# Layer 0's output projection: four of six chunk pairs as block products over all 16 k-tiles

## The chip, the core and the metric

The kernel runs as one program on one core of a Trainium2 chip. A core has five engines with queues of their own, which run in order: TensorE (PE; its weight loads are shown as PEld), VectorE (DVE), ScalarE (ACT), GpSimd (POOL) and SyncE (SP), which here does nothing but issue DMA transfers. The metric is the device time of one execution in microseconds (us); several executions are timed and the median is given. Beside them one execution was recorded by the hardware profiler; all rows below come from it.

## The reference

One step of a two-layer backbone over 640 tokens (128 context tokens, 512 latent tokens), 2048 features, fp32. Each layer normalises and modulates the input, projects it to branch inputs and gates, runs two branches (layer 0: windowed attention and gated linear attention; layer 1: neighbourhood attention and spatial gating), multiplies by the gate, and projects back:

```
for l in range(DEPTH):                       # DEPTH = 2
    shift, scale, gate = modulation(c, ada_w[l], ada_b[l])
    h = rms_norm(x, norm_g[l]) * (1.0 + scale[:, None]) + shift[:, None]
    y, _ = even_mixer(h, ...)   or   odd_mixer(h, ...)
    x = x + gate[:, None] * (y @ w_out[l])   # w_out[l]: 2048 x 2048
y_sample = rms_norm(x, final_norm_g)
```

The change concerns `y @ w_out[0]` alone.

## The kernel before, in words

**Layout.** Activations are feature-major: a tensor of 2048 features by 640 tokens is 16 k-tiles of 128 partitions x 640 columns. The tokens fall into two halves of 320. Every fp32 operand is split into a high and a low part in a reduced fp32 format (`acth`/`actl` for activations, `whi`/`wlo` for weights), and each fp32 product is three matmuls: high x high, low x high, high x low. Weights arrive raw (`wraw`, `rs`), ScalarE writes `whi`, GpSimd or now and then VectorE writes `wlo`, four k-tiles (128x512) at a time, into a ring that holds five such units.

**The output projection** has 16 output chunks of 128 features. Chunks 0 and 1 are done as a plain pair (`kpair`, 2 x 16 k-tiles x 2 halves x 3 = 192 matmuls). Chunks 2 to 13 are six pairs done by `spair`. Chunks 14 and 15 are a plain pair again, which in layer 0 runs into layer 1's input projection.

**Block products.** A pair has 2 chunks x 2 k-halves (k-tiles 0 to 7 and 8 to 15) on the weight side and 2 k-halves x 2 token halves on the activation side, a 2x2 by 2x2 block product. `spair` forms it with 7 products instead of 8 (Strassen's scheme): four of them use sums of activations (f = 0, 1, 2, and `t3`, which overwrites the second token half of `acth`/`actl` for k-tiles 0 to 7), four use sums of weight blocks (S1 to S4), which VectorE forms in `rs`/`wraw`. There are two forms:

- The full form (`ns` = NS = 8): all 16 k-tiles in block products; 7 products x 8 k-tiles x 3 = 168 matmuls, 14 weight units, 8 sums of 128x512 on VectorE.
- The short form (`ns` = NR = 4): k-tiles 0 to 3 and 8 to 11 in block products, 4 to 7 and 12 to 15 plainly; 7 x 4 x 3 + 4 units x 4 k-tiles x 2 halves x 3 = 84 + 96 = 180 matmuls, 11 weight units, 4 sums.

The order of a pair's steps (`steps`, line 656):

```
todo = "A11' A11 A12 A12' S1' S1 S4' S4 S2 S2' S3 S3' A22 A22'".split()      # full, first of a row
return [*names("A11"), *a[:1], *names("A12"), *a[1:], *names("S1", "S2", "S4"), *b[:1], *names("S3"), *b[1:], *names("A22")]   # short
```

A prime means the far half of the k-tiles; a and b are the plain units of the two chunks.

**Near and far sums.** `fold` prepares the activation sums. The near ones (k-tiles 0 to 3 with 8 to 11) are made by VectorE and kept on chip in `eh`/`el`. The far ones (4 to 7 with 12 to 15) are made by GpSimd and ScalarE (`far` in `fold`), stored to `far_dram`, and read back one sum at a time into four slots in `tail`; the slots lie where k-tiles 12 to 15 of the residual `Y` would be, and `turn_tail` swaps the two uses. When a product has read a slot for the last time, the transfer that brings the slot's next sum is issued (`far_load`). `t3` and the overwritten halves of `acth`/`actl` go through DRAM as well (`t3_dram`, shown as `t_dram`; `bh_dram`, `bl_dram`): `third` in `fold` brings `t3` in, `unfold` restores the old content for the plain pair that follows. If `fold` gets no third flag, it makes no far sums and all this is done for k-tiles 0 to 3 alone.

**What sets the order.** The program is written out by a planner in Python: `Pace` keeps an estimated clock for each engine; while TensorE's matmuls are written in fixed order, pending work of the other engines (evacuations, splits, weight sums, fold steps) is put into their queues when the planner thinks that its inputs are there. All DMA transfers go through SP's queue. A background task, `ada_task`, computes the modulation vectors (`part`, `partg`) from 64 weight tiles of 128x2048 (`ada`) on VectorE, piece by piece through four buffers `adas`, wherever the planner sees room; its outputs are needed by layer 1's input (jobs `s1`, `1`) and by layer 1's output projection (job `g1`).

The pairs are formed in `program`; `pairs(n, short, used)` marks the first `short` of `n` pairs as short and gives the last short one the flag `used`, which tells `fold` that k-tiles 4 to 7 are no longer read plainly:

```
acts.extend(("s", [c[2 * i], c[2 * i + 1], NR if i < short else NS, used if i == short - 1 else None, None]) for i in range(n))
pairs((KT - 4) // 2, SHORT[l], f"us{l}")
```

Layer 1's output projection already has two short pairs and four full ones, with a fold that makes far sums.

Of the kernel before, what the change touches and what calls it, by code (L numbers as in the profile page):

```python
# [41 lines left out]
LEAD, FIRST = 2, 8  # L42
ORDER = "k0 v0 q0 q1 k1 v1 q2 q3 g0 q4 q5 g1 q6 g2 q7".split()
GHOSTS = 12, 13
SHORT = 6, 2


class Pace:
# [187 lines left out]
class Trunk:  # L236
# [2099 lines left out]
    def program(self):  # L2336
# [23 lines left out]
        def pairs(n, short=0, used=None):  # L2360

            c = [acts.pop()[1] for _ in range(2 * n)][::-1]
            acts.extend(("s", [c[2 * i], c[2 * i + 1], NR if i < short else NS, used if i == short - 1 else None, None]) for i in range(n))

        def do(f):
            acts.append(("f", f))
# [203 lines left out]
        def to_y(l, free, cs):  # L2570

            for k in ORDERS[l]:
                y = self.yt(k) if l else Y[:, k, :]
                yield from self.wait(f"{free}:{k}", *(f"evac{c}" for c in cs if k in ORDERS[l][-2:]))
                yield from self.until(y)
                yield from self.calm(self.calms[0])
                self.act_plain(k, y, f"y{l}:{k}")
                yield

        def out_proj(l, xsrc, sp):  # L2580
            for i, f in enumerate(range(KT)):
# [4 lines left out]
                elif i == KT - 3:  # L2586
                    pairs((KT - 4) // 2, SHORT[l], f"us{l}")
            do(lambda: self.turn_tail(False))
# [10 lines left out]
        cs = pair("k", ORDERS[0], None, "fe")  # L2599
        k = acts.pop()  # L2600
        do(lambda: self.spawn(to_y(0, "fe", cs)))
        do(lambda: self.fold("y0", "uo0", None))
        acts.append(k)
        do(lambda: (self.need("ada_g0"), self.spawn(scales())))

# [456 lines left out]
```

## Time and profile before

| | us |
|---|---|
| three timed executions | 2086.84, 2087.51, 2090.91 (median 2087.51) |
| profiled execution | 2084.72 |
| its span, first to last instruction | 2082.9 |
| TensorE busy in the span | 2036.0 (98%) |
| layer 0's output projection, about | 840 to 1031 |
| layer 1's output projection, about | 1850 to 2070 |

The profiled execution spends 1.8 us outside the span. A stretch is named by microseconds from the span's start. "Busy" of TensorE counts overlapping matmuls once; a matmul of 320 columns is recorded with some 310 ns, but the next one starts 147 ns later. In a list of waits each row gives who waited, for whom, the total, how often, and the longest.

### The profile page before, as it was taken

The numbers are of one execution on the slowest core, as the hardware profiler recorded it, in microseconds if no ns is written. First come the engines' busy times: TensorE is split into PE (matmuls) and PEld (weight loads), VectorE is DVE, ScalarE is ACT, GpSimd is POOL, SyncE is SP. The second block draws the span as 40 slices with busy tenths as digits, with TensorE's granted clock in tenths as the row PEclk, the third lists the DMA queues.
The fourth block names the chain that finished last, engine by engine and source line by source line (L and its number), as shares of the span: only waits on it lengthen the run. The fifth ranks groups of instructions, "written<-read, shape, count | busy, mean of one in ns | idle before, by whom it ended". The sixth has DMA issues, their size and how long they took to land. (4 is left out here: it accounts for less than half of the span.)

```text
span 2082.9 us, 38915 instructions
## 1 busy us (share of the span) xinstructions
PE 2036.0 (98%) x13930; PEld 1963.8 (94%) x13930; DVE 1503.7 (72%) x3465; ACT 959.6 (46%) x1995; POOL 1097.9 (53%) x830
## 2 busy tenths in 40 slices
PE   7999999999999999999999999999999999999996
PEld 4788999999999999999999999999999999999995
DVE  1447788887888777788767778987785667676465
ACT  3344444353334454544454544555554545454443
POOL 3447243233222223466556675756666567658783
PEclk9999999999999999999999999999999999999998
DMA  9954333345554434776648856756665575567756
GB/s 374 359 173 134 124 119 124 122 137 184 159 169 142 128 127 132 232 253 221 205 132 274 269 192 231 253 198 213 219 197 192 179 258 190 191 222 244 249 186 217
DMA packets 215874, 412.52 MB, mean 198 GB/s; under 512 B 25664, under 2 KB 88320, under 8 KB 215680
## 3 DMA queue, kind: packets, MB, share of 16 engines
q1 hardware_dynamic: 214208, 408.43, 58.9%
q8 instruction: 109, 1.79, 0.3%
q10 hardware_dynamic: 1472, 1.61, 0.2%
q14 instruction: 85, 0.70, 0.1%
HBM read 368.88 MB, written 38.45 MB: 196 GB/s over the span
## 5 line engine op out<-in xcount | busy, mean ns | idle before, releaser
L396 PE MATMUL bank<-acth,whi 128*128 128x320 f32 (+1 forms) x3112 | 956.8, 319 | 8.8 <-DVE arena L210 3.0
L396 PE MATMUL bank<-acth,wlo 128*128 128x320 f32 (+1 forms) x3112 | 929.9, 311 | 3.3 <-POOL wlo L210 3.1
L396 PE MATMUL bank<-actl,whi 128*128 128x320 f32 (+1 forms) x3112 | 928.8, 310 | 0.0
L210 POOL TENSOR_TENSOR wlo<-wraw,whi 128x512 fp32r<-128x512 f32 x363 | 505.5, 1399 | 663.5 <-ACT whi L210 596.1
L396 PEld LDWEIGHTS bank<-acth,whi 128*128 128x128 f32 x3112 | 578.9, 189 | 26.1 <-issue 11.2
L396 PEld LDWEIGHTS bank<-acth,wlo 128*128 128x128 f32 x3112 | 578.6, 189 | 4.7 <-POOL wlo L210 4.6
L396 PEld LDWEIGHTS bank<-actl,whi 128*128 128x128 f32 x3112 | 579.0, 189 | 1.8
L210 POOL TENSOR_TENSOR wlo<-rs,whi 128x512 fp32r<-128x512 f32 x292 | 407.5, 1408 | 185.2 <-ACT whi L210 162.3
L210 ACT ACTIVATE whi<-wraw 128x512 fp32r<-128x512 f32 x393 | 241.0, 624 | 163.0 <-PE bank L396 87.4
L210 ACT ACTIVATE whi<-rs 128x512 fp32r<-128x512 f32 x329 | 201.1, 625 | 104.2 <-PE bank L396 60.9
L210 DVE CUSTOM_DVE_ANT_0 adas<-adas,bank,partg 128x256 bf16<-128x256 f32 (+1 forms) x320 | 178.0, 556 | 19.2 <-DMA adas<-ada_g 10.0
L396 PE MATMUL bank<-tail,whi 128*128 128x322 f32 (+1 forms) x672 | 152.0, 313 | 0.1
L210 ACT ACTIVATE arena<-arena,bc 128x128 f32<-128x128 f32 (+3 forms) x167 | 83.6, 519 | 143.7 <-DVE bc L210 95.2
L396 PE MATMUL bank<-eh,whi 128*128 128x322 f32 (+1 forms) x444 | 138.8, 313 | 0.0
L396 PE MATMUL bank<-el,whi 128*128 128x322 f32 (+1 forms) x444 | 137.8, 310 | 0.0
L396 PE MATMUL bank<-eh,wlo 128*128 128x322 f32 (+1 forms) x444 | 137.7, 310 | 0.0
L210 DVE TENSOR_TENSOR bank<-bank,sums 128x320 f32<-128x320 f32 (+1 forms) x162 | 76.6, 493 | 66.9 <-PE bank L396 58.5
L210 ACT ACTIVATE Y<-bank 128x128 f32<-128x128 f32 (+5 forms) x134 | 52.2, 411 | 138.8 <-PE bank L396 73.0
L210 ACT ACTIVATE sums<-bank 128x320 f32<-128x320 f32 (+1 forms) x125 | 54.5, 436 | 127.3 <-PE bank L396 118.9
L396 PEld LDWEIGHTS bank<-tail,whi 128*128 128x128 f32 x672 | 112.2, 189 | 0.5 <-DMA tail<-far_dram 0.4
L210 DVE TENSOR_TENSOR rs<-rs 128x512 f32<-128x512 f32 x83 | 85.5, 1036 | 31.8 <-POOL wlo L210 31.4
L396 PE MATMUL bank<-tail,wlo 128*128 128x322 f32 (+1 forms) x336 | 103.8, 309 | 0.0
(227 smaller groups left out, 2870.5 us busy)
## 6 DMA issues: line engine op xcount, KB each, us to landing
tail<-far_dram SPq DMA_DIRECT2D x196, 322.0 KB, 4.0
wraw<-w_even SPq DMA_DIRECT2D x176, 256.0 KB, 3.1
adas<-ada_g SPq DMA_DIRECT2D x128, 256.0 KB, 3.8
adas<-ada SPq DMA_DIRECT2D x128, 256.0 KB, 3.7
rs<-w_odd SPq DMA_DIRECT2D x63, 512.0 KB, 5.7
wraw<-w_odd SPq DMA_DIRECT2D x37, 512.0 KB, 5.6
more<-ada SPq DMA_DIRECT2D x36, 512.0 KB, 7.5
rs<-w_out SPq DMA_DIRECT2D x30, 512.0 KB, 5.7
```

The source lines that it names most:

```text
L210: return f(*args, **kw)
L396: self.nc.tensor.matmul(out, lhsT, rhs, start=start, stop=stop, **kw)
```

## The change

The table entry `SHORT` for layer 0 goes from 6 to 2, and layer 0's `fold` gets the flag `us0` as its third argument, so that it makes far sums:

```
-SHORT = 6, 2
+SHORT = 2, 2
...
-        do(lambda: self.fold("y0", "uo0", None))
+        do(lambda: self.fold("y0", "uo0", "us0"))
```

The third to sixth pairs (chunks 6 to 13) become full. The instructions of the planner's other work move with them.

GpSimd's queue at the start of layer 0's output projection, while chunks 0 and 1 are multiplied (`Y` and `tail` hold the gated branch outputs there, `stage` is a buffer of the fold):

```order
-L210 TENSOR_TENSOR wlo<-wraw,whi 128x512 x151
-L210 TENSOR_TENSOR wlo<-rs_7760,whi 128x512
-L210 TENSOR_TENSOR wlo<-wraw,whi 128x512 x2
+L210 TENSOR_TENSOR wlo<-wraw,whi 128x512 x146
+L210 TENSOR_TENSOR Y<-Y 128x320
+L210 TENSOR_TENSOR Y<-tail_81,Y 128x320
+L210 TENSOR_TENSOR wlo<-wraw,whi 128x512
+L210 TENSOR_TENSOR Y<-Y,stage_7761 128x320
+L210 TENSOR_TENSOR tail_81<-tail_81,Y 128x320
+L210 TENSOR_TENSOR wlo<-wraw,whi 128x512
```

The far sums (128x320) stand between the low parts of the weights; there are 32 of them, spread over the plain pair and the two short pairs, where before there was none.

SP's queue in the third pair (`tail<-far_dram` are the slots' next sums, `rs` and `wraw` the weights, `adas` the background task):

```order
+L434 DMA tail_8872<-far_dram 128x2x320 x2
+L434 DMA adas<-ada 128x512
+L434 DMA rs_7760<-w_out 128x1024
 L434 DMA adas<-crow_s 128x512 x2
-L434 DMA adas<-ada 128x512 x3
+L434 DMA rs_7760<-w_out 128x1024
+L434 DMA tail_8872<-far_dram 128x2x320 x2
+L434 DMA adas<-ada 128x512
+L434 DMA tail_8872<-far_dram 128x2x320 x2
+L434 DMA wraw<-w_out 128x1024
+L434 DMA rs_7760<-w_out 128x1024
+L434 DMA adas<-ada 128x512 x2
```

The slot transfers stand between the weights and the background task's pieces, of which fewer are left in this stretch.

## Rows read from the trace of the kernel before

**Rows 1.** The page, part 1: busy us, share of the span, instructions.

```profile
PE 2036.0 (98%) x13930; PEld 1963.8 (94%) x13930; DVE 1503.7 (72%) x3465; ACT 959.6 (46%) x1995; POOL 1097.9 (53%) x830
```

**Rows 2.** Windows: stretch, length, busy (count) by engine, clock, DMA share, GB/s.

```profile
core 0: us, PE busy (x) PEld busy (x) DVE busy (x) ACT busy (x) POOL busy (x), PEclk, DMA share, GB/s
860.00:1030.00 170.00, 170.00 (x1156) 170.00 (x1155) 134.42 (x383) 76.08 (x147) 111.43 (x91) 1.00 0.72 231
...
1864.00:1940.00 76.00, 76.00 (x519) 76.00 (x518) 46.07 (x67) 34.23 (x70) 62.96 (x55) 1.00 0.77 250
1940.00:1960.00 20.00, 19.36 (x129) 18.76 (x129) 10.13 (x15) 7.07 (x13) 15.93 (x12) 1.00 0.76 241
1960.00:2040.00 80.00, 80.00 (x546) 79.97 (x545) 48.38 (x63) 35.58 (x69) 63.12 (x49) 1.00 0.68 222
```

**Rows 3.** Windows: the background task beside layer 1's attention heads, and the heads alone.

```profile
1300.00:1560.00 260.00, 259.62 (x1757) 255.01 (x1756) 212.99 (x623) 132.31 (x295) 166.61 (x122) 1.00 0.64 218
1560.00:1700.00 140.00, 140.00 (x948) 137.57 (x947) 87.89 (x205) 72.93 (x159) 81.66 (x62) 1.00 0.61 209
```

**Rows 4.** Windows: 20 us with the DMA engines full.

```profile
1100.00:1120.00 20.00, 20.00 (x137) 20.00 (x136) 7.91 (x14) 5.73 (x12) 9.09 (x9) 1.00 0.99 342
```

**Rows 5.** TensorE's waits, 1864 to 2040.

```profile
PE bank L396 <- ACT sums L210: 0.5, 1, 0.5
```

**Rows 6.** TensorE's waits, 1045 to 1090.

```profile
PE bank L396 <- DVE tail L210: 2.4, 2, 1.9
PE bank L396 <- POOL wlo L210: 0.4, 1, 0.4
```

**Rows 7.** DMA, 860 to 1030: queue, packets, MB, share; then issues, KB, us to landing.

```profile
q1 hardware_dynamic: 21028, 38.97, 71.7%
...
adas<-ada SPq DMA_DIRECT2D x34, 256.0 KB, 4.6
...
adas<-ada_g SPq DMA_DIRECT2D x19, 256.0 KB, 4.2
...
adas<-crow_s SPq DMA_DIRECT2D x7, 256.0 KB, 4.7
```

**Rows 8.** DMA, 1864 to 2040.

```profile
q1 hardware_dynamic: 26018, 41.36, 72.2%
...
tail<-far_dram SPq DMA_DIRECT2D x36, 320.0 KB, 4.3
...
far_dram<-Y SPq DMA_DIRECT2D x12, 160.0 KB, 3.4
```

**Rows 9.** Transfers to and from `far_dram`, 1864 to 2040: ns min/median/max, first and last start.

```profile
L434 SPq DMA_DIRECT2D tail<-far_dram x36: 359/419/1076, 1920.2 to 2018.0; - x36
...
  PEld bank L396: 0.4, 1
...
DMA to landing us min/median/max: 1.9/4.0/7.3
```

**Rows 10.** TensorE in order of time, layer 1's first full pair.

```profile
1947.63 0.46 PE L396 MATMUL bank<-tail,whi 128*128 128x320 f32 x2
```

**Rows 11.** VectorE by form, 1864 to 2040: busy us, mean ns, idle before.

```profile
L210 DVE TENSOR_TENSOR rs<-rs 128x512 f32<-128x512 f32 x13 | 14.8, 1147 | 13.3 <-POOL wlo L210 13.2
L210 DVE TENSOR_TENSOR wlo<-rs,whi 128x512 fp32r<-128x512 f32 x14 | 14.3, 1030 | 8.2 <-ACT whi L210 8.1
```

**Rows 12.** The background task on VectorE, 860 to 1030: ns min/median/max, first and last start.

```profile
L210 DVE CUSTOM_DVE_ANT_0 adas<-adas,bank,part x74: 735/748/751, 870.9 to 959.4; 128x512 bf16<-128x512 f32 x74
```

**Rows 13.** The same, 1400 to 1800.

```profile
L210 DVE CUSTOM_DVE_ANT_0 adas<-adas,bank,partg x71: 462/476/484, 1404.0 to 1552.1; 128x256 bf16<-128x256 f32 x71
```

## The prediction

> **What bounds the kernel now.** The page's busy shares come first: TensorE is busy for 98% of the span, no other engine for more than 72% [rows 1]. The window over layer 0's output projection, where the change lies, says more: in 860 to 1030 TensorE is busy for all of 170 us, at the full clock, with 1156 matmuls, so one every 170/1156 = 0.1471 us [rows 2]. A matmul less there is worth 0.147 us as long as nothing else becomes late. The others have room, but not much: VectorE 134 of 170 us, GpSimd 111, the DMA engines 72%. The third look is at a twin: layer 1's output projection already has two short and four full pairs. In 1864 to 2040 TensorE stands still there for 0.64 us in all, in the one window 1940 to 1960 [rows 2], and the list of waits has one entry, 0.5 us [rows 5]. The twin lacks what layer 0 has beside it, the background task of modulation vectors: in 860 to 1030 that task brings 34 + 19 + 7 pieces of 256 KB [rows 7].
>
> **Matmuls, -7.1 us.** A short pair has 180 matmuls, a full one 168. Four pairs by 12 by 0.1471 us [rows 2] is 7.06 us. The order of the changed program has 48 matmuls fewer, so the change does what it says, and I give no chance to its doing nothing. The weight loads go with their matmuls.
>
> **The first full pair, +1.1 us.** The twin has 129 matmuls in 1940 to 1960, and 546 in the 80 us behind it, 136.5 in 20 us [rows 2]: 7.5 fewer, 1.1 us. TensorE waits there for a copy of ScalarE to free a bank [rows 5] and for a slot transfer, 0.4 us on the weight-load queue [rows 9]. Layer 0's third pair gets the same steps, so I take the same: bounds 0 (there is only this one such place) and 2.2 (both waits twice as long).
>
> **The fold of the far sums, 0.** 32 subtractions of 128x320 come on GpSimd, with their splits on ScalarE and 32 stores. What they must not miss is the third pair's first product with a slot. In the twin the first slot transfer is issued at 1920.2 [rows 9] and the first matmul that reads a slot starts at 1947.63 [rows 10]: 27 us of cover. In layer 0 the same steps stand between the same pairs, with the background task's pieces among them. If the cover is gone, each us later costs one; more than 27 us I do not expect.
>
> **VectorE and GpSimd, 0.** A full pair needs four more weight sums and three more weight units than a short one: 16 sums and 12 units in all, a sum at 1147 ns and a low part on VectorE at 1030 ns [rows 11]. The order gives VectorE 13 low parts more and GpSimd one fewer over the whole program, so VectorE gets 16 x 1.15 + 13 x 1.03 = 32 us of work more. What gives way is the background task: of its operations in this stage the order keeps 82, where 143 stood. The 61 that leave are of the shorter kind, 61 x 0.48 = 29 us [rows 13]. VectorE's load in the stage stays about where it is. GpSimd has 32 subtractions more, near 1 us each, on 111 of 170 us: about 80%, and the twin has 63 of 76 and 63 of 80 us, with TensorE standing still for 0.64 us [rows 2]. Zero, then, with 2 us as the upper bound (five waits for a low part of 0.4 us [rows 6]).
>
> **The DMA engines, +3.3 us.** This is where I see the doubt. 38.97 MB at a share of 71.7% in 170 us [rows 7] is 320 GB/s with the engines full; the twin's 41.36 MB at 72.2% in 176 us [rows 8] gives 325. The change adds, by the order: 36 slot transfers of 328 KB (11.8 MB), 24 stores of far sums, 8 of `t3`, and 8 each way of the two saved and restored halves and of `t3` coming in, 164 KB each, some 9 MB; it takes away 17 pieces of 262 KB (4.5 MB). Before, the stage moved 231 GB/s x 191 us = 44 MB; now about 60 MB in 190 us, 317 GB/s. The engines go from 72% to nearly full. Counted by pair, the second asks for 8.8 MB, the third for 9.7, the sixth for 10.0; at 322 GB/s a short pair's 26.5 us carry 8.5 MB and a full one's 24.7 us 8.0. The excess is 0.3, 1.7 and 2.0 MB, or 0.8 + 5.4 + 6.3 = 12.5 us late, if nothing were loaded ahead. That is the upper bound. The lower one is 0: at 1100 to 1120 the DMA share was 0.99 at 342 GB/s and TensorE did not miss a matmul [rows 4], because weights are loaded a pair ahead. What is not far ahead is a slot: it may be loaded only when its last reader is done, and in the third pair it is read again soon after; a landing in the twin took 4.0 us at the median and 7.3 at most [rows 9]. I take one such late landing, 3.3 us.
>
> A page of the Trainium skill would say otherwise: HBM Reference, Specifications (TRN2), states that a core streaming alone measures about 425 GB/s. At that rate, an estimate, the third pair's 9.7 MB would need 22.8 us of its 24.7, this term would be 0 and the sum -5.0 + 0 instead of the one below. The rows' 320 to 342 GB/s with the engines full speak against it for this mix of pieces.
>
> **The background task comes later, +0.7 us.** 74 operations of its job `1` end at 959.4 [rows 12]; in the order they end in the sixth pair, some 50 us later by that pair's place. Layer 1's input needs them one plain pair further on, 192 x 0.147 = 28 us: covered. The last job, `g1`, ends at 1552.1 [rows 13]; the order has its last piece some 130 us later by its place, just before the heads' stretch is over. There VectorE has 88 of 140 us to do, and 31 us come on top: 85%. With task and heads together in 1300 to 1560 it had 213 of 260, 82%, and TensorE lost 0.38 us, against 0.00 in the stretch without the task [rows 3]. Scaled to 140 us that is 0.2; with five waits for a low part [rows 6] it would be 2.2. I take 0.7, nearer the low end.
>
> The wait at the start of layer 1's input, 2.4 us behind VectorE [rows 6], stays; it depends on what VectorE holds at that moment and may shrink or grow by as much. I take 0.
>
> **The sum.** -7.06 + 1.1 + 3.3 + 0.7 = -2.0 us. The profiled execution, 2084.7 us (1.8 us of it outside the span), would become 2082.7. It lies 2.8 us under the median of the three timed ones; against that median, 2087.5, the forecast is 2085.5.
>
> **Rivals.** First, *the gain is kept*: the transfers are loaded ahead far enough and the later task costs 0.2. Then -7.06 + 1.1 + 0.2 = -5.8, or 2081.7. For it: the 20 us at 0.99 [rows 4], and the twin's 0.64 us. Against it: here the engines would be nearly full for 190 us, not for 20. This is also the case in which the skill's rate for a lone core would hold.
>
> Second, on the other side, *DMA becomes the bound of the third and sixth pairs*: all that exceeds 322 GB/s is late and TensorE waits for slots, `t3` and weights. The price is the 12.5 us above: -7.06 + 1.1 + 12.5 + 0.7 = +7.2, or 2094.7. It decides as soon as the excess costs more than about 7 us before it is caught up. For it: pieces of the background task share the queue and sit between the slot transfers. Against it: in the fourth and fifth pairs, with some 7.5 MB each, there is room to catch up, and the planner's own rule puts a piece of the task in only when the buffer before it is used up.
>
> Third, *the modulation comes too late*: if VectorE is so far behind that job `1` ends more than 28 us after the sixth pair, layer 1's input waits. 8 us beyond that would give -2.0 + 8 = +6, or 2093.5. The row speaks for the room: the operations are 748 ns each and 82 of them stand in 160 us.
>
> **How the numbers follow.** 0.2% of this kernel is 4.2 us, about what a measurement of it can tell from no change. The gain is kept (under 2083.3): 0.27. The sum, with the DMA term between 1.5 and 9 us: 0.55. Slower by more than 4.2 us: 0.18, of which 0.13 DMA, 0.05 the modulation. The largest gain that can be had, with the wait behind VectorE gone too, is about 8 us; the range stops at -6.0, 2081.5, since a full kept gain with a lucky wait is under 1 in 10. On the other side it stops at +4.5, 2092.0, between the sum and the DMA rival's full price, again with some 1 in 10 above.
>
> **What would show each step.** 48 matmuls fewer between 840 and 1031 and the start of layer 1's input some 3 us earlier than 1059 if the sum holds, 6 us earlier if the gain is kept, later if DMA binds. The DMA share over the stage above 0.9; under 0.85 my demand is wrong. Waits of TensorE (or its weight loads) for `tail<-far_dram` in the third pair: one of some 3 us, none, or several with waits for `wraw`/`rs` behind them. Job `g1` ending near 1690 and no new waits for `wlo` in 1560 to 1700. The forecast is wrong in its reasons if the time is lost behind GpSimd's or VectorE's queue with the DMA engines idle.

## The result, and the profile after

The changed kernel takes 2100.27 us (median of 5 runs, 2095.95 to 2102.17) beside 2087.51 for the kernel before (5 runs, 2086.66 to 2093.52): a ratio of 1.0054, 95% interval 1.0040 to 1.0068. By that ratio it is slower by 11 us. Repeated later beside other kernels it gave 1.0043 (1.0029 to 1.0056). Forecast were 2085.5 us and a range of 2081.5 to 2092.0.

The profiled execution takes 2102.17 us, with a span of 2100.1 against 2082.9. The page's first part, which answers to [rows 1], shows the 48 matmuls gone and VectorE and GpSimd busier:

```profile
PE 2038.4 (97%) x13882; PEld 1962.3 (93%) x13882; DVE 1553.6 (74%) x3494; ACT 972.5 (46%) x2027; POOL 1135.0 (54%) x861
```

To see where the time went I worked out from the matmul records of each trace what TensorE lost in a stretch: the time from each matmul's start to the next one's, less the median of that time for its shape, summed. Waits count in it, and matmuls that run at a lower clock. In us:

```
stretch                      before   after   after, repeated
up to 840                      76.6    80.3    76.3
840 to 920                      2.1     2.6     2.6
920 to 960  (third pair)        0.0     8.0     7.3
960 to 1040 (to the sixth)      0.2     3.3     2.0
1040 to 1110 (start of input)   6.2     9.8     9.8
1110 to 1740                    4.0     9.1    10.0
from 1740                      10.8    11.2     9.7
sum                            99.9   124.3   117.8
```

The sum grows by 24.4 us, the matmuls give back 7.1: 17.3, the difference of the spans (17.2). Up to 840 both kernels run the same program; the 3.7 us there are how executions differ, and the repeated profile does without them: 17.9 - 7.1 = 10.8, close to the timed difference. What has to be explained are three places: 9 to 11 us in the projection, 3.6 at the start of layer 1's input, 5 to 6 behind it. Each column is one execution. Two kernels below, `early_g1` and `after_fs`, have the instructions of after in this order up to 1045; with them four executions of one program lost 7.3 to 9.3 us in 920 to 960 and 9.4 to 13.2 in 920 to 1040.

**The projection.** The windows (the stretch, its length, busy time and count by engine, granted clock, DMA share, GB/s) answer to [rows 2, 3]:

```profile
860.00:1030.00 170.00, 164.43 (x1081) 161.83 (x1080) 143.95 (x274) 82.93 (x168) 136.75 (x110) 0.98 0.92 307
870.00:920.00 50.00, 50.00 (x341) 50.00 (x341) 41.96 (x90) 26.80 (x56) 43.99 (x41) 1.00 0.99 329
920.00:960.00 40.00, 35.48 (x220) 33.66 (x219) 31.82 (x59) 15.45 (x31) 26.11 (x20) 0.95 0.88 301
1300.00:1560.00 260.00, 259.61 (x1756) 254.79 (x1755) 216.54 (x608) 130.08 (x288) 164.36 (x120) 1.00 0.64 215
1560.00:1700.00 140.00, 138.19 (x935) 135.34 (x934) 113.87 (x329) 75.43 (x164) 81.46 (x61) 1.00 0.64 211
```

The DMA engines went from 0.72 to 0.92 over the stage and have nothing free from 870 to 920. TensorE still misses nothing there; it does in the next 40 us, where 220 matmuls stand instead of some 272. The DMA view of 860 to 1030, beside [rows 7]:

```profile
q1 hardware_dynamic: 31234, 52.01, 91.1%
...
tail<-far_dram SPq DMA_DIRECT2D x36, 320.0 KB, 5.0
adas<-ada SPq DMA_DIRECT2D x34, 256.0 KB, 5.9
x1T_dram<-Y SPq DMA_DIRECT2D x12, 320.0 KB, 6.1
```

13 MB more move in the same 170 us, and a background piece takes 5.9 us to land instead of 4.6. TensorE's waits in 920 to 960 (total, times, longest):

```profile
PE bank L396 <- ACT whi L210: 1.6, 1, 1.6
PE bank L396 <- DMA tail<-far_dram: 1.3, 3, 0.9
PE bank L396 <- POOL wlo L210: 1.1, 1, 1.1
PE bank L396 <- ACT sums L210: 0.5, 1, 0.5
```

The slots that the prediction looked at are 1.3 us of 4.5. The larger part are split weights, and the timelines say why they were late: SyncE's queue first, then ScalarE's (start, duration, instruction, idle time before it).

```profile
920.80 0.33 SPq L434 DMA_DIRECT2D far_dram<-tail  x1
924.96 1.41 SPq L434 DMA_DIRECT2D tail<-far_dram  x3
926.41 0.47 SPq L434 DMA_DIRECT2D x1T_dram<-Y  x1
926.98 0.38 SPq L434 DMA_DIRECT2D adas<-ada  x1
```

```profile
922.31 0.63 ACT L210 ACTIVATE whi<-rs 128x512 fp32r<-128x512 f32 x1
932.16 1.01 ACT L210 ACTIVATE Y<-Y,A 128x128 f32<-128x128 f32 x2 [9.23 <-DMA x1T_dram<-Y]
933.08 0.45 ACT L210 ACTIVATE arena<-Y 128x320 f32<-128x320 f32 x1
933.44 0.61 ACT L210 ACTIVATE whi<-rs 128x512 fp32r<-128x512 f32 x1
```

SyncE comes to the first slot load when the last far sum has not landed in DRAM, and stands 3.8 us. Behind it waits the store of an output chunk. The scaling of that chunk in place is next on ScalarE, which stands 9.2 us for the store; the splits of the next weights stand behind the scaling, and GpSimd's low parts behind the splits. From 932.5 to 934.1 TensorE has none.

Most of the rest of the 8.0 us is the clock. The windows after the waits:

```profile
934.00:938.00 4.00, 2.81 (x10) 2.54 (x11) 2.27 (x4) 2.77 (x7) 4.00 (x4) 0.71 1.03 390
938.00:942.00 4.00, 4.00 (x25) 4.00 (x25) 3.93 (x11) 2.81 (x6) 4.00 (x4) 0.87 0.78 251
942.00:946.00 4.00, 4.00 (x29) 4.00 (x28) 3.96 (x9) 1.00 (x2) 4.00 (x4) 1.00 0.92 263
```

After 2.7 us of waits the granted clock is 0.71 and 0.87 for 8 us, part of them at 1.2 GHz; after the slot waits, from 958 to 966, it is 0.69 and 0.88. (0.29 + 0.13 + 0.31 + 0.12) x 4 is 3.4 us, some of it behind 960. In 920 to 960 the granted clock is 0.95, which is 2.0 us of 40; with the 4.5 us of waits 6.5 of the 8.0 are told, the rest is not in the list of waits.

**The start of layer 1's input.** TensorE's waits from 1045 to 1100, the answer to [rows 6], then ScalarE's longest wait in 1045 to 1072, and a store of 24 KB with its time from issue to landing:

```profile
PE bank L396 <- DVE tail L210: 5.0, 1, 5.0
PE bank L396 <- POOL wlo L210: 0.8, 1, 0.8
```

```profile
ACT whi L210 <- DMA wraw<-w_odd: 5.9, 1, 5.9
```

```profile
L434 SPq DMA_DIRECT2D far_dram<-fs x1: 628/628/628, 1050.5 to 1050.5; - x1
...
DMA to landing us min/median/max: 7.8/7.8/7.8
```

VectorE's chain hangs on ScalarE, and ScalarE on the first weights of layer 1's input, which land at 1062.3, after that store (1058.4), though issued at 1054.6. Before, the store was issued at 1038.7 and the same weights landed at 1049.3. So the store comes 11.8 us later than before, where TensorE itself is 8.2 later by the table (94.2 - 78.9 - 7.1): the 3.6 between them are what is lost here more than before (in the repeated profile 7.3 and 2.2, so 5.1).

**Behind it.** The background task on VectorE, in 840 to 1060 and 1400 to 1800, beside [rows 12, 13], and TensorE's waits from 1620 to 1740:

```profile
L210 DVE CUSTOM_DVE_ANT_0 adas<-adas,bank,part x74: 731/742/750, 875.2 to 1029.7; 128x512 bf16<-128x512 f32 x74
```

```profile
L210 DVE CUSTOM_DVE_ANT_0 adas<-adas,bank,partg x140: 461/477/482, 1400.9 to 1701.7; 128x256 bf16<-128x256 f32 x140
```

```profile
PE bank L396 <- POOL wlo L210: 1.4, 3, 0.8
PE bank L396 <- ACT Y L210: 0.5, 1, 0.5
```

Job `1` ends 70 us later than before and `g1` 150. Where it now overlaps the heads the low parts of weights come late: 3.7 us are lost in 1620 to 1740, 0.3 before.

### The profile page after: what moved, and what is told of

Its sections match the earlier page's. It is cut to its first block, busy times and chain, and to the rows that moved or that the text cites. A ratio compares the mean times of both kernels' runs of the same rounds, so it can differ in the third digit from the quotient of the medians.

```text
span 2100.1 us, 39058 instructions
## 1 busy us (share of the span) xinstructions
PE 2038.4 (97%) x13882; PEld 1962.3 (93%) x13882; DVE 1553.6 (74%) x3494; ACT 972.5 (46%) x2027; POOL 1135.0 (54%) x861
## 5 line engine op out<-in xcount | busy, mean ns | idle before, releaser
L396 PE MATMUL bank<-acth,whi 128*128 128x322 f32 (+1 forms) x3048 | 939.3, 320 | 17.3 <-DVE arena L210 7.3
L396 PE MATMUL bank<-acth,wlo 128*128 128x322 f32 (+1 forms) x3048 | 912.5, 311 | 6.9 <-POOL wlo L210 6.5
L396 PE MATMUL bank<-actl,whi 128*128 128x322 f32 (+1 forms) x3048 | 910.6, 311 | 0.0
L210 POOL TENSOR_TENSOR wlo<-wraw,whi 128x512 fp32r<-128x512 f32 x353 | 495.1, 1409 | 644.9 <-ACT whi L210 601.0
L396 PEld LDWEIGHTS bank<-acth,wlo 128*128 128x128 f32 x3048 | 568.0, 189 | 10.5 <-POOL wlo L210 10.1
L396 PEld LDWEIGHTS bank<-actl,whi 128*128 128x128 f32 x3048 | 568.6, 190 | 2.0
L210 POOL TENSOR_TENSOR wlo<-rs,whi 128x512 fp32r<-128x512 f32 x301 | 422.3, 1417 | 189.1 <-ACT whi L210 162.1
L396 PE MATMUL bank<-tail,whi 128*128 128x322 f32 (+1 forms) x768 | 174.8, 315 | 2.2 <-DMA tail<-far_dram 2.2
L396 PEld LDWEIGHTS bank<-tail,whi 128*128 128x128 f32 x768 | 129.6, 190 | 3.5 <-DMA tail<-far_dram 3.5
L396 PE MATMUL bank<-tail,wlo 128*128 128x322 f32 (+1 forms) x384 | 119.6, 311 | 0.9 <-POOL wlo L210 0.9
```

Of the source, the lines that this page charges most:

```text
L210: return f(*args, **kw)
L396: self.nc.tensor.matmul(out, lhsT, rhs, start=start, stop=stop, **kw)
```

## The experiments

Ratios are to the kernel before on the same chip, with the 95% interval. "Lost" is the measure of the table.

**How many full pairs.** The line is `SHORT = 6, 2`, `5, 2`, `4, 2` or `3, 2` in the kernel after; with 6 this is added:

```
-            self.deep = NS if far_used else NR
+            self.deep = NS if far_used and far_used != "us0" else NR
```

> The far block sums are made, split and stored in DRAM as in the kernel after, but all six pairs stay short and none of them uses a far sum, so that no slot is reloaded and the 48 matmuls of before are back. Theory A (the time is lost where full pairs draw their slots beside DMA engines that have nothing free): the sums by themselves cost little, 2088 to 2092 us. Theory B (the time is lost to the making of the sums: more work in the in-order queues of VectorE, ScalarE, GpSimd and SyncE, and a background task that ends later): the loss of 20 us stays and the 7 us of matmuls are missing, 2098 to 2108 us.

> Five pairs short, only the sixth full: 12 matmuls fewer than before (1.8 us). Theory A: the sixth pair draws its slots where the DMA engines were busy for 0.51 of the time before, so the pair gains nearly its matmuls: 2086 to 2090 us. Theory B: 2096 to 2106 us, as for the sums alone less 1.8.

> Four pairs short, the fifth and sixth full: 24 matmuls fewer than before (3.5 us), and the third pair, where the kernel after lost 9 us, is short again. Theory A: 2084 to 2090 us. Theory B: 2095 to 2104 us.

> Three pairs short, the fourth to sixth full: 36 matmuls fewer (5.3 us), one full pair fewer than the kernel after. Theory A, if it is the first full pair's place right behind the making of the sums that costs: 2083 to 2092 us; if every full pair costs the same, 2095 to 2098. Theory B: 2093 to 2102 us.

Measured: the sums alone 2090.74 us (1.0020, 1.0011 to 1.0029); one full pair 2099.57 (1.0060, 1.0047 to 1.0072); two 2096.02 (1.0045, 1.0033 to 1.0058); three 2096.74 (1.0056, 1.0042 to 1.0070). Neither theory fits: the sums alone cost 4 us, as A said, but a single full pair, the sixth, makes it 13, as B said, and more of them make it no worse. In `short5` the third pair is short and 5.5 us are lost in 920 to 960 all the same. Up to 999 its instructions are those of `sums_only`, in the same order, and that lost 2.3 there: so far apart are two executions. In both TensorE has one wait in this stretch, for VectorE's sums, 2.0 us in `sums_only` and in `short5`:

```profile
PE bank L396 <- DVE sums L210: 3.7, 1, 3.7
```

These sums wait for a copy on ScalarE, whose queue had stood for a chunk's store, as in after, and then 1.5 us for a load of the background task. The longest waits of `short5` from 920 to 950, ScalarE's and then SyncE's:

```profile
ACT Y L210 <- DMA x1T_dram<-Y: 7.1, 2, 5.4
```

```profile
SPq L434 <- DMA far_dram<-tail: 3.6, 1, 3.6
```

So much of what the third pair loses it loses not because it is full but because it stands beside the making of the sums: 2.3 to 5.8 us in the four kernels where it is short, 7.3 to 9.3 in the four executions where it is full.

**The order on SyncE's and ScalarE's queues.** `far_wait` adds the first two lines ahead of the slots' use, `scale_wait` the third behind the wait for a chunk's store:

```
+            if shift is None and far_used == "us0":
+                yield 5.0
             self.flags.add("Tf")
...
                 yield from self.wait(f"sp{k}")
+                yield 6.0
```

> The kernel after, with the first four slot loads of the third pair put 5 us later in the written order, so that on SyncE's queue the store of an output chunk (x1T_dram<-Y) and a background load stand ahead of them. In the profile of after SyncE stood 3.8 us at the first of these loads until the last far sum had landed in DRAM, the chunk's store behind it landed at 932.1, ScalarE waited 9.2 us for it with the weights' splits queued behind, and TensorE lost 4.7 us between 920 and 940. Theory A (this in-order chain SyncE, store, ScalarE is what the third pair lost): the loss at 920 to 940 falls to under 2 us, the time by 2 to 4 us to 2096 to 2098. Theory B (the DMA engines are full there and any order loses the same): no change, 2099 to 2101 us.

> The kernel after, with each scaling of an output chunk on ScalarE (Y<-Y,A) put 6 us later, so that the chunk's store has more time to land before ScalarE's queue reaches an instruction that waits for it. Theory A (ScalarE's queue standing at such a scaling is what holds the weights' splits): the 9.2 us wait of ScalarE for x1T_dram<-Y goes, TensorE's 4.7 us at 920 to 940 shrink to under 2, 2095 to 2098 us. Theory B (full DMA engines): the weights are late anyway, 2099 to 2101 us.

Measured: 2088.79 (0.9998, 0.9983 to 1.0012) and 2091.47 (1.0016, 0.9999 to 1.0033). Both gain more than A said, `far_wait` the whole 11 us. But its lost time fell only from 7.3 to 5.7 in 920 to 960, with slots late instead of splits (TensorE's waits there):

```profile
PE bank L396 <- DMA tail<-far_dram: 1.9, 3, 1.5
PE bank L396 <- ACT sums L210: 0.5, 1, 0.5
```

Of 10.4 us that it lost less than the repeated profile of after, 6.5 lie in 1110 to 1740 (3.5 for 10.0). The planner writes every later instruction anew when one moves, and `g1` ends at 1654 instead of 1698. So the next experiment moves the loads and nothing else: each DMA goes through `issue`, which holds the three back until two others have passed.

```
-            self.nc.sync.dma_start(out, in_)
+            self.issue(out, in_, swap)
...
+                self.swap = far_used == "us0" and i < 3
                 self.far_load(i, 0, shift is not None)
```

> The kernel after itself, unchanged, beside the other kernels of this group: both theories expect 9 to 13 us over before (ratio 1.004 to 1.006).

> The kernel after with one thing moved on SyncE's queue and nothing on any other engine: the first three slot loads (tail<-far_dram) stand behind the next chunk store (x1T_dram<-Y) and the next background load instead of ahead of them. Theory A (the chain SyncE waiting for far sums to land, chunk store late, ScalarE standing at the scaling that waits for this store, splits late): the loss at 920 to 960 (8.0 us in after) falls by 3 to 5 us and the time with it, 4 to 6 us under after. Theory B (what made the kernel with the later loads 12 us faster than after is the other order that the planner then wrote on all engines): at most 1 us under after.

Measured, on one chip: after 2096.53 (1.0043, 1.0029 to 1.0056), `swap` 2094.25 (1.0036, 1.0024 to 1.0048). ScalarE's wait for the store shrinks to 3.2 us at most, TensorE no longer waits for high parts, and waits more for slots (its waits from 920 to 960):

```profile
PE bank L396 <- DMA tail<-far_dram: 2.0, 4, 0.9
PE bank L396 <- POOL wlo L210: 0.9, 1, 0.9
PE bank L396 <- ACT sums L210: 0.5, 1, 0.5
```

In 920 to 960 5.2 us are lost instead of 7.3 to 9.3, in 920 to 1040 8.7 instead of 9.4 to 13.2. The chain is there, but its price is 2 to 4 us in its place and 0.7 to 4.5 over the projection; by time the two can't be told apart. The rest of what `far_wait` gained then came with another order of later work; which part of that order is not shown.

**The DMA load.** `no_loads` leaves out every load of the jobs `1` and `g1`, in the whole program:

```
             if i < len(todo):
+                name = next(x[2][0] for x in todo[i:] if not isinstance(x[2], list))
+                if name in ("1", "g1"):
+                    return
                 self.dma(todo[i][0](raws[i % 4]), todo[i][1])
```

> The kernel after without the background task's loads for layer 1's shift and gate (34 loads of 256 KB between 870 and 1041 us left out, its VectorE work kept, so those modulation values are not computed from the weights). Theory A (a late chunk store and late slots are what the third pair lost, both because the DMA engines were full): 3 of 9 MB less there, the loss at 920 to 960 falls from 8.0 to under 3 us, 2094 to 2097. Theory C (VectorE's and GpSimd's queues are what is late): the loss stays at 7 to 9 us.

Measured: 2087.70 (1.0003, 0.9994 to 1.0012), 9 us under after. The windows 870 to 920 and 920 to 960, and TensorE's waits in the latter:

```profile
870.00:920.00 50.00, 50.00 (x342) 50.00 (x341) 45.30 (x98) 28.05 (x59) 45.31 (x43) 1.00 0.79 260
920.00:960.00 40.00, 39.00 (x262) 38.21 (x262) 38.20 (x80) 18.00 (x36) 28.20 (x22) 1.00 0.89 285
```

```profile
PE bank L396 <- ACT sums L210: 0.5, 1, 0.5
PE bank L396 <- POOL wlo L210: 0.5, 1, 0.5
```

VectorE is busier there than in after (38.2 of 40 us for 31.8) and 1.8 us are lost instead of 7.3: theory A, against C. The clock stays at 1.00. In 960 to 1040 2.6 us are lost, no fewer than in the repeated profile of after (2.0). And the planner wrote another order here too, on ScalarE and VectorE from some 885 us on, so the gain need not be the load's alone.

**The loads moved instead of left out.** `early` on after, `early_before` on before; `early_best` is `early` with `far_wait` and the late store of the next part:

```
-    rooms, calms, lags = (0.5, 1.2, 1.5, 0.8), (4.0, 2.0), (3.0, 3.0, 2.0, 1.0, 0.4)
+    rooms, calms, lags = (2.0, 2.5, 1.5, 1.6), (4.0, 2.0), (3.0, 3.0, 2.0, 1.0, 0.4)
...
-                yield
+                yield 200.0 if last[0][0] == "1" else 0.0
```

> The kernel after with the background task given more room on VectorE before the output projection and none in it: its job for layer 1's shift is to be done by about 845 us instead of 1030, the gate's job then rests until about 1045 and goes on from there with more room. Nothing is left out. Theory A (the third pair and the start of layer 1's input lose time because the DMA engines are full there): no background loads stand between 870 and 1040, the loss at 920 to 960 falls from 7.3 to under 3 us as it did without these loads, and the time to 2085 to 2092. Theory C (VectorE's queue): the same gain here, but with the losses moved ahead of 840, where VectorE then has more to do (over 80 us lost there instead of 76), 2092 to 2098.

> The same with the slot loads 5 us later and the 24 KB store behind the first weight loads of layer 1's input. If the three parts add up: 6 to 10 us under after, 0 to 5 us under before (2081 to 2086). If the DMA load was the whole of it: as the kernel with the early task alone.

> The kernel before with the same early background task, to see what that is worth where no far sums are made: theory A: within 2 us of before, since before lost nothing at 920 to 1040. Were it faster by more than 3 us, the task's place would be worth something by itself.

Measured: 2114.76 (1.0141, 1.0126 to 1.0157), 2106.57 (1.0097, 1.0081 to 1.0114) and, for the control, 2113.67 (1.0134, 1.0121 to 1.0148). All three lose 100 us instead of 76 ahead of the projection, mostly in waits behind VectorE between 240 and 580; theory C had named this place, but not a price of this size. Against its control the change now costs 1.1 us instead of 10, which the intervals don't tell from nothing. With the two repairs of order it is 7.1 us faster than the control; some 3.7 of these are the late store's, which the control lacks (lost at the start of layer 1's input: 10.7 in `early`, 7.0 in `early_best`, 7.4 in the control). The program runs 24 us later, so the third pair stands in 944 to 984. There `early` still loses 5.7 us, not the under 3 of theory A, with the DMA engines at 0.77 and VectorE at 23.7 of 40 us. Its window, TensorE's waits in it for slots, and ScalarE's for chunk stores from 930 to 984:

```profile
944.00:984.00 40.00, 36.90 (x236) 34.34 (x235) 23.69 (x29) 16.50 (x34) 28.42 (x24) 1.00 0.77 254
```

```profile
PE bank L396 <- DMA tail<-far_dram: 1.6, 4, 0.9
```

```profile
ACT Y L210 <- DMA x1T_dram<-Y: 12.8, 4, 6.2
```

`early_best`, whose slot loads come 5 us later, has one wait of TensorE there, 0.5 us, and loses 1.0 (the control 0.0):

```profile
PE bank L396 <- ACT sums L210: 0.5, 1, 0.5
```

Over the projection, 920 to 1040 or 944 to 1064, that makes 9.4 to 13.2 us lost with the load and after's order (after), 7.7 with the later slots alone (`far_wait`), 5.8 with the load moved alone (`early`) and 1.1 with both (`early_best`). Neither the full DMA engines nor the order of the queues is the whole cause; the loss goes when both are gone.

**The store ahead of layer 1's first weights.** One line in `shifts`, on after, on before, and on `far_wait`:

```
+            yield 50.0
             e = self.far.rearrange("p i f a b -> p (i f a) b")[:, :, 0:2]
```

> The kernel after, with the 24 KB store far_dram<-fs (7.8 us from issue to landing in after) put behind the first weight loads of layer 1's input instead of ahead of them. Theory A (TensorE's wait of 5.0 us at the start of layer 1's input is that for the first load of w_odd, which lands right behind this store): the wait falls to under 2 us and the time by 3 to 5 us, to 2095 to 2097. Theory B (the wait follows the last chunks' chain of VectorE and ScalarE): it stays at about 5, 2099 to 2101 us.

> The kernel before, with the same store put behind the first weight loads of layer 1's input. Theory A: the waits of 1.9 and 0.5 us at the start of layer 1's input shrink, by 1 to 3 us in all, to 2083 to 2085 against a kernel before of 2086 to 2087. Theory B: no change.

> The kernel after with both: the slot loads 5 us later in the written order, and the 24 KB store behind the first weight loads of layer 1's input. If the two losses are separate, the 12 us of the first and some 3 us of the second add up: 2 to 4 us under before (ratio 0.998 to 0.999). If either only moves a wait to a later place, the same as before.

Measured: `after_fs` 2095.12 (1.0022, 1.0008 to 1.0036), `before_fs` 2087.35 (0.9987, 0.9974 to 1.0001), `wait_fs` 2087.36 (1.0001, 0.9990 to 1.0012). TensorE's waits from 1045 to 1100 in `before_fs` and, its line for the same chain, in `after_fs`:

```profile
PE bank L396 <- DVE tail L210: 1.7, 1, 1.7
```

```profile
PE bank L396 <- DVE tail L210: 0.6, 1, 0.6
```

The loss in 1040 to 1110 falls by 3.1 us in after (9.8 to 6.7) and by 3.3 in before (6.2 to 2.9): the wait is for the weights behind that store, theory A. It explains the wait, not that it grew by 3.6: that difference remains with the store moved (6.7 to 2.9). `sums_only`, which brings back 4 pairs of saved half blocks ahead of that store as before does, loses 7.2 in 1040 to 1110, and `short3` to `short5`, which bring back 8 as after does, 10.1 to 13.9. In time the gain on before is not settled, and in `wait_fs` it does not add to that of `far_wait`: 13.7 us are lost from 1740 on, for 8.8.

**The background task's end.**

```
-    rooms, calms, lags = (0.5, 1.2, 1.5, 0.8), (4.0, 2.0), (3.0, 3.0, 2.0, 1.0, 0.4)
+    rooms, calms, lags = (0.5, 1.2, 1.5, 1.6), (4.0, 2.0), (3.0, 3.0, 2.0, 1.0, 0.4)
```

> The kernel after with more room for the background task in layer 1's input alone, so that the gate's job ends near 1575 us as in before instead of 1700. If its late end is what is lost at 1620 to 1740 (3.1 to 3.7 us in after, 0.3 in before), that loss goes to under 0.6 and the time falls by 2 to 4 us, unless the work is lost between 1110 and 1620 instead (5.4 to 6.9 us there in after, 3.6 in before): then the same as after.

Measured: 2096.93 (1.0051, 1.0039 to 1.0064), no gain. `g1` ends at 1572 and 0.5 us are lost in 1620 to 1740 instead of 3.1 to 3.7, with 6.8 in 1110 to 1620 where after lost 5.4 and 6.9. At the ordinary pace the loss in 1620 to 1740 follows the job's end: 0.3 to 0.4 us in the kernels where it ended by 1611, 1.0 to 1.2 at 1651 to 1656, 3.1 to 3.7 at 1693 to 1702. So by the trace the late end costs some 3 us and moving it sooner saves them; the time, at 1.0051 beside 1.0054 and 1.0043, shows nothing of it.

**A version that should beat both.** `mild_best` is `wait_fs` with rooms of (1.0, 1.2, 1.5, 1.6) and a rest of 100.0, `mild_before` before with the late store and the same task.

> The kernel after with the slot loads 5 us later, the 24 KB store behind the first weights of layer 1's input, and the background task moved only a little: somewhat more room on VectorE in the first third of the program (1.0 for 0.5), so that the job for layer 1's shift ends some 40 us sooner, a rest of 100 us behind it, and more room in layer 1's input. If the losses of the change are the full DMA engines and the order on SyncE's queue, and the mild move costs under 3 us ahead of 840 (the strong one cost 24): 2 to 6 us under before, 2081 to 2085 beside 2086.6. If the strong move's price is not avoided: 2086 to 2095.

> The kernel before with the same background task and the same late store, as the control: within 3 us of before. If the change by itself then gains what its 48 matmuls take, this kernel is 4 to 7 us slower than the one with the change; if the third pair's loss stays, they are equal.

Measured: 2089.58 (1.0021, 1.0008 to 1.0033) and 2084.63 (0.9994, 0.9984 to 1.0004). It beats neither, and with the task still in the projection the change costs 5 us against its control (lost in 920 to 1040: 7.6 and 0.3). Its window over the third pair shows the DMA engines as full as ever:

```profile
920.00:960.00 40.00, 37.24 (x245) 35.84 (x245) 34.88 (x67) 18.35 (x38) 29.65 (x23) 1.00 1.00 351
```

## Why the prediction was wrong

**Matmuls, -7.1 us: right.** 13930 - 13882 = 48, and the sum of the losses less 7.1 gives the difference of the spans.

**The DMA engines, +3.3 us, with the first full pair's +1.1: the step that failed.** The demand was foreseen well (317 GB/s and nearly full; measured 307 at 0.92, 329 at 0.99). The size and the place were not: 9 to 11 us in 920 to 1040 where 4.4 were forecast. "One such late landing" of a slot took the slot for the only transfer that is not far ahead. A chunk's store is another: it frees nothing that TensorE reads, but ScalarE's in-order queue stands for it with the weights' splits behind, and SyncE's queue put it behind a load that waits. The 4.5 us of waits also brought 3.4 us at the lower clock. The load is one half of the cause: without a part of it 4.4 us are lost in 920 to 1040 (`no_loads`, with another order too), with it moved 5.8 (`early`). The order on the queues is the other half: with the later slots as well 1.1 are left (`early_best`), with them alone 7.7 (`far_wait`). How much of it is the chunk's store is open; `swap`, which moves that alone, saved 2 to 4 us in 920 to 960. The twin [rows 2, 8] lacked both the load and the chunk stores on this queue; I named the first and priced it too low.

The Trainium skill's HBM Reference, Specifications (TRN2), by which this term would have been 0, is not borne out for this mix of transfers: with the engines at 0.99 and 1.00 they moved 329 and 351 GB/s (870 to 920 in after, 920 to 960 in `mild_best`), not 425. In the first 105 us of after they moved 372 at 0.98. The sum by that rate is given as -5.0 in the prediction; its terms, -7.06 + 1.1 + 0.7, make -5.3.

**VectorE and GpSimd, 0: right in the main. The fold, 0: wrong by 4 us.** `no_loads` has more VectorE work in the stretch and loses little. Waits for low parts in the sixth pair came to 0.9 us, under the 2 of the bound. The cover that the fold was judged by held: the first matmul that reads a slot starts at 938.6, 14 us after the first slot load, and does not wait for it. But the making of the sums by itself costs 4 us (`sums_only`), with 2.3 us in 920 to 960 (5.5 in `short5`), through ScalarE's and SyncE's queues; part of the 9 to 11 us above is this term's.

**The wait at the start of layer 1's input, taken as 0: +3.6 us.** I put it down to what VectorE holds. It is the first weights of that layer behind a small store, by `before_fs` and `after_fs`. Why the change makes it longer was not tested by itself; in the trace twice as many saved half blocks (8 pairs of loads for 4) stand on SyncE's queue between the last projection loads and that store, and the kernels with 8 lose more there than the one with sums and 4.

**The background task, +0.7 us: some 3, at most 5 to 6.** Its end was foreseen (1690; measured 1702), its price was not: some 3 us where it meets the heads in 1620 to 1740, which `early_g1` and the ends of the job in the other kernels show. Some 2.5 more were lost in 1110 to 1620; that they are the task's is not shown, and `before_fs`, the kernel before with one store moved, lost 6.5 there for 3.6.

**The rivals.** The second, DMA as the bound, was the nearest: +7.2 in all for the 11 measured, with 12.5 + 1.1 us for the DMA engines and the first full pair where 9 to 11 were lost, through weights more than through slots. It got 0.13, because TensorE had missed nothing in 20 us with full engines [rows 4]; after, it missed nothing in the first 50 such us either, and then did. The third did not happen: TensorE did not wait for the modulation. "Lost behind GpSimd's or VectorE's queue with the DMA engines idle", the sign that would have refuted the reasons, is half there, for 1110 to 1740, with the engines at 0.64 from 1300 on.

## What to carry to other kernels

A stretch of full DMA engines that costs nothing says little about a longer one: count how long the demand stays above what they move, and then look for every transfer whose landing an in-order engine waits for, stores too, not only for what TensorE reads. On an in-order issue queue a load that must wait for a store to land holds up all that stands behind it, so what does not wait belongs ahead of it. Where a planner orders the program, compare against a control with the same side conditions, and do one move in the written order by hand: one delayed step here changed the time by several times the price of the chain that it mended. And read more than one profile before a few us are put down to a cause: the same instructions lost 2.3 us and 5.5 us in the same 40.

## What the runs showed of the hardware

Waits of 1.6 and 1.1 us within 4 us were followed by a granted clock of 0.71 and 0.87 in the 8 us from 934 on, and slot waits of 0.2, 0.9 and 0.2 us within 3 us by 0.69 and 0.88: 4.5 us of waits went with 3.4 us lost to the clock.

A store of 24 KB in 3072 pieces of 8 bytes took 6.7 to 9.2 us from issue to landing in the twenty profiles (7.8 in after), and the transfers issued next behind it landed after it in all of them. The Trainium skill (DMA: Bandwidth & Descriptors, Bandwidth) says that transfers under 64 KB are dominated by their descriptors; the trace agrees: a load of 256 KB on the same queue landed in 3.1 us in `before_fs`, where this store had been moved, and in 9.9 us in before, right behind it.
